# Opening, low parts and closing of a one-layer hybrid encoder: packed first loads, a set operand order, fewer column sums

## The chip, the cores and the metric

The kernel runs on one core of a Trainium2 chip. The metric is the device time of one execution in microseconds. The time before is the median of three runs.

## The reference

One encoder layer over x of 512 positions by 1024 channels, all in float32. What is computed:

```python
def rms_norm(x, g):
    y = xf * lax.rsqrt(jnp.mean(xf * xf, axis=-1, keepdims=True) + EPS)
    return y * g

def swiglu(h, w_gate, w_up, w_down):
    return (jax.nn.silu(h @ w_gate) * (h @ w_up)) @ w_down

x = x + 0.5 * swiglu(rms_norm(x, ffn1_norm), ffn1_w_gate, ffn1_w_up, ffn1_w_down)   # F = 2752
h = rms_norm(x, mix_norm)
u = h @ w_in                       # fourier 512 | q 8x64 | k 2x64 | v 2x64
f_out = fourier_mixer(u[..., :512], fnet_w, fnet_b)
a_out = gqa_attention(q, k, v, q_norm, k_norm)
x = x + jnp.concatenate([f_out, a_out], axis=-1) @ w_out
x = x + 0.5 * swiglu(rms_norm(x, ffn2_norm), ffn2_w_gate, ffn2_w_up, ffn2_w_down)
return rms_norm(x, final_norm)
```

## The kernel before

x is kept transposed in SBUF for the whole run: eight tiles `x[k]` of 128 channels by 512 positions. Every product is made of three matmuls on rounded operands: a number is split into a high part (a rounding copy to fp32r) and a low part (the rest), and `product` (L107 to L110) adds high by high, high by low and low by high into one PSUM bank. ScalarE (ACT in the profile) makes most high parts, VectorE (DVE) most low parts (`lows`, L71). Where `rest_by_dma` is used (L89 to L92), ScalarE writes the negated high part, and a DMA queued on GpSimd (POOL) adds the source to it while it transfers.

The weights stay in DRAM and are loaded by DMAs that SyncE (SP) issues in the order of the program. The raw buffers of tag `raw` (three) and `raw_g` (two) are used in turn, so a load waits for the engine that last read its buffer.

**Order.** TensorE (PE) and SP keep the order of the program (`manual_schedule` in `in_order`, L63). ScalarE, VectorE and GpSimd get theirs from a scheduler, which places each instruction by its own estimate of time; on the chip each engine then runs its queue in that order and each instruction waits for its semaphores.

**Opening** (`opening1`, L546 to L566). Eight warm-up matmuls on zeros (`WARM`, L519) run while the first loads are under way. The norm weights `gains` come by a DMA on ScalarE's queue (L56), x in five transfers and the first gate and up weights in five (`raw_first`, L525 to L531); two small tables, `qkg` and `fb`, come by DMAs on GpSimd's queue (L542, L544). Then, for pairs of channel blocks k, `scale` makes the high and low part of x times the norm weight (`hh[k]` at L125 or L127, `hl[k]` at L128), the raw weights are split (L553, L71), and the twelve matmuls of a k go through four banks `gu0_0` to `gu0_3`, three per bank in turn. The squares for the norm (`square` at L134, `sums` at L140) are added into `acc`. Ahead of k = 6 PE takes the column sum of `acc` (`sum`, L157), ahead of k = 7 it spreads the result over the rows (`row`, L184). The norm itself is applied later, when the banks are read (`evacuate`).

**Gates 42 and 4 to 7.** Five more `gate` products follow, of eight channel blocks and 24 matmuls each: 42, which is the tail, then 4, 5, 6 and 7. The tail's down weights (`tail_weights`, `rawt`, L230 to L239) are loaded and split in the same time. The low parts of the weights of gates 4 to 7 are made by `rest_by_dma`. Between them `operands` (L244 to L262) makes seven operands `rt` for the next stage from tiles `b` and `t`, for i = 0 to 3; in the first FFN the low parts of the three taken from `b` are made by `rest_by_dma` too. The `b` tiles share the two `raw_g` buffers.

**Middle.** The down products of four groups (`down`), a seven-product scheme for the rest of gate and up (`seven`, L330), the projections, attention and Fourier mixer, the output projection, and the second FFN. The change does not touch these.

**Closing** (`closing`, L970 to L1014). The last three down products are made for positions 0 to 255 (`t0`) first, then for 256 to 511 (`t1`). During `t1` PE takes the column sums of the squares of `t0` (`column`, after the third step), and `finish` (after the eighth) spreads the result and scales the output of `t0`. After the last down product the column sums of `t1` follow, the mean and power of each column pair, `rows`, and `finish` for `t1`: VectorE scales six of the eight tiles (L965) and GpSimd two (`ready`, tiles 2 and 3, L963), and four DMAs on SP store pairs of tiles in the order 0, 2, 4, 6 (L968).

Of the kernel before, what the change touches and what calls it, by code (L numbers as in the profile page):

```python
# [6 lines left out]
F32 = mybir.dt.float32  # L7
F32R = mybir.dt.float32r
BF16 = mybir.dt.bfloat16
# [14 lines left out]
WARM = 8  # L24
# [18 lines left out]
def encoder(ctx, tc, A, out):  # L43
# [68 lines left out]
    class Norm:  # L112
# [9 lines left out]
        def scale(self, k, by=None):  # L122
            g = gains[:, self.n, k : k + 1]
            if by:
                by.tensor_scalar(out=hh[k], in0=x[k], scalar1=g, scalar2=None, op0=ALU.mult)  # L125
            else:
                nc.scalar.activation(hh[k], x[k], AF.Copy, scale=g)  # L127
            nc.vector.scalar_tensor_tensor(  # L128
                out=hl[k], in0=x[k], scalar=g, in1=asf(hh[k]), op0=ALU.mult, op1=ALU.subtract
            )  # L130
# [24 lines left out]
        def sum(self, ps, c, parts, first=True, last=True):  # L155
            for i, p in enumerate(parts):
                nc.tensor.matmul(  # L157
                    ps[:, 2 * c : 2 * c + 2], p[:, c * P : (c + 1) * P], ones,
                    start=first and i == 0, stop=last and i == len(parts) - 1,
                )  # L160
# [39 lines left out]
    def ffn(norm, after, wgu, wd, wdt, opening, closing):  # L200
# [6 lines left out]
        with tc.tile_pool(name=f"act{n_}", bufs=1) as ap, tc.tile_pool(name=f"sums{n_}", bufs=2) as sp:  # L207
# [36 lines left out]
            def operands(rp, i0, i1):  # L244
                for i in range(i0, i1):
# [279 lines left out]
    nc.sync.dma_start(out=x[0], in_=A["x"][:, 0, :])  # L525
    nc.sync.dma_start(out=raws[0][:, 0:2], in_=A["first"][0][:, 0:2])
    nc.sync.dma_start(out=raws[0][:, 2:4], in_=A["first"][0][:, 2:4])
    nc.sync.dma_start(out=x[1], in_=A["x"][:, 1, :])
    for i in range(1, KH):
        nc.sync.dma_start(out=xt[:, 2 * i : 2 * i + 2, :], in_=A["x"][:, 2 * i : 2 * i + 2, :])  # L530
        nc.sync.dma_start(out=raws[i], in_=A["first"][i])  # L531
# [10 lines left out]
    nc.gpsimd.dma_start(out=qkg, in_=A["qkg"])  # L542
    fb = cp.tile([P, 4], F32, name="fb")
    nc.gpsimd.dma_start(out=fb, in_=A["fb"])  # L544

    def opening1(gate, column, row):  # L546

        pss = [bank(f"gu0_{c}") for c in range(4)]
        for i in range(KH):
            n0.scale(2 * i, None if i else nc.vector)  # L550
            hi, lo = (slot().rearrange("p (c a b) -> p c a b", c=4, b=P) for _ in range(2))
            for c in (slice(0, 2), slice(2, 4)) if i == 0 else (slice(0, 4),):
                nc.scalar.copy(hi[:, c], raws[i][:, c])  # L553
                lows(lo[:, c], raws[i][:, c], hi[:, c])
            n0.scale(2 * i + 1)
            if i == KH - 1:
                for k in range(KD):
                    n0.sums(k)
            for k in (2 * i, 2 * i + 1):
                if k == KD - 2:  # L560
                    column()
                if k == KD - 1:
                    row()
                for c in range(4):
                    product(pss[c], hi[:, c, k % 2, :], lo[:, c, k % 2, :], hh[k], hl[k], k == 0, k == KD - 1)
        return [pss[0:2], pss[2:4]]  # L566
# [388 lines left out]
    def finish(c0, c1, row=n3.row):  # L955
# [3 lines left out]
        for k0 in range(0, KD, 2):  # L959
# [8 lines left out]
            nc.sync.dma_start(out=out[:, k0 : k0 + 2, t], in_=xt[:, k0 : k0 + 2, t])  # L968

    def closing(downs, residual):  # L970
# [4 lines left out]
        sqs = []  # L975
# [82 lines left out]
def _layout(i):  # L1058
# [13 lines left out]
    def down(w):  # L1072
# [6 lines left out]
    mix = np.concatenate([np.arange(512)] + [512 + h * HD + np.arange(HD) for t in range(4) for h in (t, t + 4)])  # L1079
    w_in = i["w_in"]  # L1080
    wgu1 = gate_up(i["ffn1_w_gate"], i["ffn1_w_up"])
    return {
        "x": i["x"][0][_order()].T.reshape(KD, P, S).transpose(1, 0, 2),
        "gains": np.stack(
            [i[n].reshape(KD, P).T for n in ("ffn1_norm", "mix_norm", "ffn2_norm", "final_norm")], axis=1
        ),
# [3 lines left out]
        "first": first(wgu1),  # L1090
# [31 lines left out]
```

## Time and profile before

| | |
|---|---|
| median of 3 runs | 880.9 us (880.14 to 881.03) |
| the profiled execution's own time | 880.02 us |
| its span in the trace | 878.0 us |
| granted TensorE clock over the span | 0.996 |
| PE busy | 862.1 us (98%) |
| DVE, ACT, POOL busy | 637.2, 459.6, 31.7 us |

The trace gives times from the start of the span. A busy share near 100% on PE does not say that each matmul is at its shortest; gaps in which PE waits are read from the list of waits and the timeline, where the bracket at the end of a row tells how long the engine was idle before it and for whom it waited. A row with x2 merges two instructions; its duration is from the start of the first to the end of the second.

### The profile page before, as it was taken

The page shows a single profiled execution, that of the slowest core. Times are in us where ns is not written, and L with a number is a line of the kernel's source. Part 1 is how long each engine was busy: PE and PEld are TensorE (multiplying, and loading weights), DVE is VectorE, ACT ScalarE, POOL GpSimd, SP SyncE. Part 2 cuts the span into 40 slices and gives each one's busy share as a digit, 9 for nine tenths or more (in the row PEclk, how much of TensorE's full clock was granted, in tenths as well). Part 3 has the DMA queues.
Part 4 walks back from the last instruction along what each step waited for, and adds up shares of the span by engine and source line. Part 5 has one row for each costly group of instructions (what it writes and reads, how often), then busy time and mean ns, then how long its engine had stood idle before and what let it go on. Part 6 is the DMA issues. An engine that isn't in the chain of part 4 may idle for free.

```text
span 878.0 us, 13599 instructions
## 1 busy us (share of the span) xinstructions
PE 862.1 (98%) x5394; PEld 768.8 (88%) x5394; DVE 637.2 (73%) x1005; ACT 459.6 (52%) x761; POOL 31.7 (4%) x37
## 2 busy tenths in 40 slices
PE   8999999999999999999999999999999999999996
PEld 5878998899989998888888888889998999889986
DVE  7697985488746837699888558987974688459553
ACT  7773664256524644667775445535652366326441
POOL 0210000000000000211000000000000000000001
PEclk9999999999999999999999999999999999999998
DMA  7873322323243113521110213232323232332212
GB/s 245 199 163 135 142 85 67 120 97 119 75 143 110 46 51 108 204 84 37 49 49 25 90 63 136 84 132 97 109 78 126 95 118 78 102 115 84 73 37 96
DMA packets 31328, 89.25 MB, mean 102 GB/s; under 512 B 3616, under 2 KB 9248, under 8 KB 31136
## 3 DMA queue, kind: packets, MB, share of 16 engines
q1 hardware_dynamic: 28560, 83.37, 27.9%
q0 software_dynamic: 2560, 4.99, 3.0%
q8 instruction: 42, 0.69, 0.3%
q14 instruction: 22, 0.18, 0.1%
q10 hardware_dynamic: 144, 0.02, 0.0%
HBM read 83.91 MB, written 2.10 MB: 98 GB/s over the span
## 4 chain that ended last, share of the span: by engine, by line
PE 50%; issue 39%; DVE 5%; DMA 2%; ACT 2%; POOL 0%; SPq 0%; DVEq 0%; POOLq 0%; ACTq 0%
PE r L330 11%; PE q L330 6%; PE dn L108 4%; PE dn L110 4%; PE dn L109 4%; PE p L330 3%; PE out L108 2%; PE out L110 2%; PE out L109 2%; PE gu L110 1%; PE pt L816 1%; PE gu L108 1%; PE gu L109 1%; DMA rt<-b 1%; DMA ring<-in_wgu 1%
## 5 line engine op out<-in xcount | busy, mean ns | idle before, releaser
L330 PE MATMUL r<-rt,ring 128*128 128x256 f32 x1632 | 213.2, 283 | 0.1
L330 PEld LDWEIGHTS r<-rt,ring 128*128 128x128 f32 x1632 | 201.8, 188 | 2.6 <-ACT u L338 0.3
L108 PE MATMUL dn<-at,ring 128*128 128x512 f32 x303 | 119.7, 395 | 0.0
L109 PE MATMUL dn<-at,ring 128*128 128x512 f32 x303 | 119.6, 395 | 0.0
L110 PE MATMUL dn<-at,ring 128*128 128x512 f32 x303 | 119.6, 395 | 0.0
L330 PE MATMUL q<-rt,ring 128*128 128x256 f32 x816 | 107.9, 281 | 0.0
L330 PEld LDWEIGHTS q<-rt,ring 128*128 128x128 f32 x816 | 101.6, 188 | 0.0
L416 DVE SCALAR_TENSOR_TENSOR xt<-dn,xt 128x512 f32<-128x512 f32 x61 | 41.9, 688 | 80.1 <-PE dn L110 80.1
L71 DVE TENSOR_TENSOR ring<-s,ring 128x1024 fp32r<-128x1024 f32 x68 | 82.8, 1220 | 17.8 <-PE r L330 10.8
L100 ACT CAST ring<-raw_dn 128x768 fp32r<-128x768 f32 (+1 forms) x59 | 45.5, 775 | 95.2 <-PE dn L109 80.7
L291 ACT CAST ring<-s 128x1024 fp32r<-128x1024 f32 x68 | 71.4, 1050 | 40.3 <-PE r L330 18.3
L110 PEld LDWEIGHTS dn<-at,ring 128*128 128x128 f32 x303 | 57.0, 188 | 13.6
L109 PEld LDWEIGHTS dn<-at,ring 128*128 128x128 f32 x303 | 57.0, 188 | 13.0
L108 PEld LDWEIGHTS dn<-at,ring 128*128 128x128 f32 x303 | 57.0, 188 | 13.0
L71 DVE TENSOR_TENSOR ring<-raw_dn,ring 128x768 fp32r<-128x768 f32 (+1 forms) x59 | 51.7, 879 | 6.8 <-ACT ring L100 5.8
L71 DVE TENSOR_TENSOR ring<-raw_g,ring 128x1024 fp32r<-128x1024 f32 x34 | 41.6, 1222 | 17.0 <-PE p L330 11.0
L330 PE MATMUL p<-rt,ring 128*128 128x256 f32 x408 | 53.9, 281 | 0.0
L330 PEld LDWEIGHTS p<-rt,ring 128*128 128x128 f32 x408 | 50.8, 188 | 0.0
L291 ACT CAST ring<-raw_g 128x1024 fp32r<-128x1024 f32 x34 | 35.7, 1049 | 22.4 <-PE r L330 8.0
L300 ACT CAST ring<-raw_u 128x512 fp32r<-128x512 f32 x34 | 21.1, 621 | 37.1 <-PE dn L110 17.9
L110 PE MATMUL gu<-ring 128*128 128x512 f32 x96 | 37.9, 395 | 2.6 <-DMA ring<-in_wgu 1.8
L108 PE MATMUL gu<-ring 128*128 128x512 f32 x96 | 37.9, 395 | 0.8 <-ACT ring L553 0.7
(324 smaller groups left out, 1574.0 us busy)
## 6 DMA issues: line engine op xcount, KB each, us to landing
raw_dn<-in_wd SPq DMA_DIRECT2D x48, 384.0 KB, 3.0
raw_g<-in_wgu SPq DMA_DIRECT2D x34, 512.0 KB, 3.7
raw_u<-in_wgu SPq DMA_DIRECT2D x34, 512.0 KB, 4.4
raw_gu<-in_wgu SPq DMA_DIRECT2D x14, 512.0 KB, 3.5
raw_o<-in_wo SPq DMA_DIRECT2D x8, 512.0 KB, 3.5
raw_dn<-in_wd SPq DMA_DIRECT2D x16, 192.0 KB, 2.4
raw_in<-in_wins SPq DMA_DIRECT2D x6, 512.0 KB, 3.7
raw_f<-in_winf SPq DMA_DIRECT2D x4, 512.0 KB, 3.6
```

The lines of the kernel that those rows point to most:

```text
L71: nc.vector.tensor_tensor(out=lo, in0=src, in1=asf(hi), op=ALU.subtract)
L100: nc.scalar.copy(hi[:, :n, :], raw[:, :n, :])
L108: nc.tensor.matmul(ps, whi, mhi, start=first, stop=False)
L109: nc.tensor.matmul(ps, whi, mlo, start=False, stop=False)
L110: nc.tensor.matmul(ps, wlo, mhi, start=False, stop=last)
L291: nc.scalar.copy(hi, src)
L300: nc.scalar.copy(hi, src)
L330: nc.tensor.matmul(ps, a[:, ks], b[:, i], start=first and i == 0 and o == 0, stop=i == KH - 1 and o == 2, skip_group_check=not first,)
L416: nc.vector.scalar_tensor_tensor(out=x[d][:, t], in0=ps[:, t], scalar=0.5, in1=x[d][:, t], op0=ALU.mult, op1=ALU.add)
L816: nc.tensor.transpose(pt[:, c * P : (c + 1) * P], prob[t, b, c][:, kc * P : (kc + 1) * P], ident)
```

## The change

Opening: `gains` and x become one SBUF tile `gx`. The norm weights stand at the head of x's first transfer, and each transfer of x and of the first weights reads one contiguous piece of DRAM. `qkg` and `fb` move from GpSimd's queue to SP's: in the built program `qkg` stands between the last transfer of x and the fourth of the first weights, `fb` behind that. ScalarE and VectorE follow the order of the program inside `opening1`; the casts and low parts of all the first weights are made in halves (the very first in quarters on ScalarE), and each pair's squares and their adds come one pair later. In the built program the squares of k = 6 and 7 stand on ScalarE behind the cast of `rawt`. PE takes the twelve matmuls of a k in the order high by high over the four banks, then high by low, then low by high. Seven warm-up matmuls instead of eight.

`operands`: for i = 0 and 1 the low parts from `b` are made by VectorE (`lows`) instead of `rest_by_dma`. In the built program this leaves GpSimd's queue with the low parts of gates 4, 5, 6, 7 and then those of i = 2 and 3; before, the two of i = 0 and 1 stood ahead of gate 6's, and that of i = 2 ahead of gate 7's.

Closing: all three squares of `t0` are added into `acc` by VectorE, so that the column sum there has two matmul instructions instead of six (each shows as two rows in the trace); `column` moves from the third to the fifth step, `finish` from the eighth to the ninth. The column sums of `t1` go into one bank and get one mean. Six matmuls on the identity (`awake`) stand between the last sums. The stores go in the order 0, 4, 2, 6, the one of tiles 2 and 3 from ScalarE's queue.

```diff
-WARM = 8
+WARM = 7
...
-    gains = cp.tile([P, 4, KD], F32, name="gains")
-    nc.scalar.dma_start(out=gains, in_=A["gains"])
-    xt = cp.tile([P, KD, S], F32, name="xt")
+    gx = cp.tile([P, 4 * KD + KD * S], F32, name="gx")
+    gains = gx[:, : 4 * KD].rearrange("p (n k) -> p n k", k=KD)
+    xt = gx[:, 4 * KD :].rearrange("p (k s) -> p k s", s=S)
...
-                        if src is t or n_:
+                        if src is t or i < 2 or n_:
                             lows(l, src, h)
                         else:
                             rest_by_dma(l, h, src)
...
+    cut = [0] + [4 * KD + k * S for k in (1, 2, 4, 6, 8)]
+    def load_x(i):
+        a, b = cut[i : i + 2]
+        src = A["x"][a * P : b * P].rearrange("(p n) -> p n", p=P)
+        nc.sync.dma_start(out=gx[:, a:b], in_=src)
+    load_x(0)
+    for c in range(2):
+        nc.sync.dma_start(out=raws[0][:, 2 * c : 2 * c + 2], in_=A["first0"][c])
+    load_x(1)
     for i in range(1, KH):
-        nc.sync.dma_start(out=xt[:, 2 * i : 2 * i + 2, :], in_=A["x"][:, 2 * i : 2 * i + 2, :])
-        nc.sync.dma_start(out=raws[i], in_=A["first"][i])
+        load_x(i + 1)
+        nc.sync.dma_start(out=raws[i], in_=A["first"][i - 1])
...
-    nc.gpsimd.dma_start(out=qkg, in_=A["qkg"])
-    nc.gpsimd.dma_start(out=fb, in_=A["fb"])
...
+        with tc.manual_schedule(engines={mybir.EngineType.Activation, mybir.EngineType.DVE}):
+            for i in range(KH):
+                a, b = 2 * i, 2 * i + 1
+                halves = slice(0, 2), slice(2, 4)
+                n0.scale_high(a, None if i else nc.vector)
+                for c in (0, 1, halves[1]) if i == 0 else halves:
+                    nc.scalar.copy(hi[:, c], raws[i][:, c])
+                n0.scale_high(b)
+                n0.scale_low(a)
+                for c in halves:
+                    lows(lo[:, c], raws[i][:, c], hi[:, c])
+                n0.scale_low(b)
+                if i:
+                    sums(i - 1)
+                if i == KH - 1:
+                    sums(i)
+                for k in (a, b):
+                    if k == KD - 2:
+                        column()
+                    if k == KD - 1:
+                        row()
+                    passes = [(c, w, m) for w, m in ((hi, hh), (hi, hl), (lo, hh)) for c in range(4)]
+                    if k == 0:
+                        passes = passes[0:2] + passes[4:6] + passes[2:4] + passes[8:10] + passes[6:8] + passes[10:]
...
+        nc.sync.dma_start(out=qkg, in_=A["qkg"])
+        nc.sync.dma_start(out=fb, in_=A["fb"])
...
-        for k0 in range(0, KD, 2):
+        for k0 in (0, 4, 2, 6):
...
-            nc.sync.dma_start(out=out[:, k0 : k0 + 2, t], in_=xt[:, k0 : k0 + 2, t])
+            queue = nc.scalar if k0 in ready else nc.sync
+            queue.dma_start(out=out[:, k0 : k0 + 2, t], in_=xt[:, k0 : k0 + 2, t])
...
+    def awake(n):
+        unit = ident.bitcast(BF16)
+        ps = bank("awake")
+        for _ in range(2 * n):
+            nc.tensor.matmul(ps[:, : 2 * P], unit[:, :P], unit, start=True, stop=True)
...
-            sq = n3.square(d, t0)
-            if d == downs[0][0]:
-                more(sq, t0)
-            else:
-                sqs.append(sq)
+            more(n3.square(d, t0), t0)
...
-                if i == 3:
-                    n3.column([n3.acc, *sqs], 0, 2)
-                if i == 8:
+                if i == 5:
+                    n3.column([n3.acc], 0, 2)
+                if i == 9:
                     finish(0, 2)
...
-        pss = [bank(f"ss3_{c}") for c in (2, 3)]
-        for c, pc in zip((2, 3), pss):
-            n3.sum(pc, c, [n3.acc, sq], last=False)
+        pc = bank("ss3_2")
+        for c in (2, 3):
+            n3.sum(pc, c, [n3.acc], first=c == 2, last=False, skip_group_check=True)
+        awake(1)
+        for c in (2, 3):
+            n3.sum(pc, c, [sq], first=False, last=False, skip_group_check=True)
         residual(KD - 1, ps, t1)
         sq = n3.square(KD - 1, t1)
-        for c, pc in zip((2, 3), pss):
-            n3.sum(pc, c, [sq], first=False)
-        for c, pc in zip((2, 3), pss):
-            n3.mean(pc, c, c + 1)
+        for c in (2, 3):
+            n3.sum(pc, c, [sq], first=False, last=c == 3, skip_group_check=True)
+        awake(2)
+        n3.mean(pc, 2, 4)
```

The host's layout function packs the inputs to match; no arithmetic of the layer is moved there.

More of the change, by code (lines that the diff above doesn't have):

```diff
@@ L127, in scale, with scale_low @@
                 nc.scalar.activation(hh[k], x[k], AF.Copy, scale=g)
+        def scale_low(self, k):
+            g = gains[:, self.n, k : k + 1]
             nc.vector.scalar_tensor_tensor(
@@ L153, in column, with sum @@
             self.spread(c0, c1)
-        def sum(self, ps, c, parts, first=True, last=True):
+        def sum(self, ps, c, parts, first=True, last=True, **how):
             for i, p in enumerate(parts):
@@ L158, in sum @@
                     ps[:, 2 * c : 2 * c + 2], p[:, c * P : (c + 1) * P], ones,
-                    start=first and i == 0, stop=last and i == len(parts) - 1,
+                    start=first and i == 0, stop=last and i == len(parts) - 1, **how,
                 )
@@ L541, in encoder, with sums @@
     qkg = cp.tile([P, 2], F32, name="qkg")
-    nc.gpsimd.dma_start(out=qkg, in_=A["qkg"])
     fb = cp.tile([P, 4], F32, name="fb")
-    nc.gpsimd.dma_start(out=fb, in_=A["fb"])
     def opening1(gate, column, row):
         pss = [bank(f"gu0_{c}") for c in range(4)]
[L549 to L558, printed above, removed]
-            for k in (2 * i, 2 * i + 1):
[L560 to L565, printed above, removed]
+        def sums(i):
+            for k in (2 * i, 2 * i + 1):
+                n0.sums(k)
@@ L974, in closing @@
         t0, t1 = slice(0, S // 2), slice(S // 2, S)
-        sqs = []
         def more(sq, t):
@@ L1079, in _layout @@
     mix = np.concatenate([np.arange(512)] + [512 + h * HD + np.arange(HD) for t in range(4) for h in (t, t + 4)])
+    x = np.concatenate(
+        [
+            *(i[n].reshape(KD, P).T for n in ("ffn1_norm", "mix_norm", "ffn2_norm", "final_norm")),
+            i["x"][0][_order()].T.reshape(KD, P, S).transpose(1, 0, 2).reshape(P, KD * S),
+        ],
+        axis=1,
+    )
     w_in = i["w_in"]
@@ L1082, in _layout @@
     return {
[L1083 to L1086, printed above, removed]
+        "x": np.concatenate([p.reshape(-1) for p in np.split(x, [4 * KD + k * S for k in (1, 2, 4, 6)], axis=1)]),
         "qkg": np.stack([np.concatenate([i[n][half]] * 2) for n in ("q_norm", "k_norm")], axis=1),
@@ L1089, in _layout @@
         "fw": i["fnet_w"].transpose(1, 0, 2).reshape(P, S),
-        "first": first(wgu1),
+        "first": first(wgu1)[1:],
+        "first0": first(wgu1)[0].reshape(P, 2, 2, 2, P).transpose(1, 0, 2, 3, 4),
         "wgu1": wgu1,
```

16 lines of the change are left out of this document (11 added, 5 removed).

## The prediction

> **What bounds the kernel now.** I read the page first, then PE's list of waits, then the timeline of the stages that the change touches.
>
> ```profile
> PE 862.1 (98%) x5394; PEld 768.8 (88%) x5394; DVE 637.2 (73%) x1005; ACT 459.6 (52%) x761; POOL 31.7 (4%) x37
> ```
>
> PE is busy for 98% of the span, so an edit counts only where it takes a PE gap away, takes instructions off PE, or shortens what lies ahead of PE's first and behind its last matmul. The change does all three. In the first 90 us PE waited for this:
>
> ```profile
> PE gu L110 <- DMA ring<-in_wgu: 1.8, 1, 1.8
> ...
> PE gu L110 <- DVE ring L71: 0.7, 1, 0.7
> PE gu L108 <- ACT ring L553: 0.7, 1, 0.7
> ```
>
> The last two lie in the opening, the first is gate 7's. PE's rows of the opening:
>
> ```profile
> 1.23 3.58 PE L520 MATMUL busy<-idle 128*128 128x512 bf16 x8 [1.23 <-DVE halves L536]
> 5.46 0.51 PE L108 MATMUL gu<-ring 128*128 128x512 f32 x1 [0.65 <-ACT ring L553]
> ...
> 7.54 0.50 PE L108 MATMUL gu<-ring 128*128 128x512 f32 x1
> ...
> 13.59 0.50 PE L110 MATMUL gu<-ring 128*128 128x512 f32 x1 [0.73 <-DVE ring L71]
> 13.93 0.39 PE L108 MATMUL gu<-ring 128*128 128x512 f32 x1
> 14.16 0.40 PE L109 MATMUL gu<-ring 128*128 128x512 f32 x1
> ...
> 24.32 0.95 PE L157 MATMUL ss<-ones,acc 128*128 128x2 f32 x8
> ```
>
> A fed matmul of 512 columns starts 0.23 us after the one before it (13.93 to 14.16), and 0.34 after one that had waited (13.59 to 13.93). The column sum stands behind 72 matmuls, so fed without a gap from 5.46 it would stand at 5.46 + 72 x 0.23 = 22.0. It stands at 24.32: the gaps cost 2.3 us. From there PE runs without a gap to gate 7.
>
> **The opening, by unchanged landings.** What feeds PE:
>
> ```profile
> 3.08 0.43 SPq L531 DMA_DIRECT2D raw_first<-in_first  x1
> 4.79 0.62 ACT L553 CAST ring<-raw_first 128x512 fp32r<-128x512 f32 x1
> 6.87 0.62 ACT L553 CAST ring<-raw_first 128x512 fp32r<-128x512 f32 x1 [1.46 <-DMA raw_first<-in_first]
> 9.59 1.41 DVE L128 SCALAR_TENSOR_TENSOR ring<-xt,gains,ring 128x512 fp32r<-128x512 f32 x2
> 10.00 1.14 ACT L134 ACTIVATE sq<-xt 128x512 f32<-128x512 f32 x2
> 12.32 1.22 DVE L71 TENSOR_TENSOR ring<-raw_first,ring 128x1024 fp32r<-128x1024 f32 x1
> 20.18 0.69 DVE L140 TENSOR_TENSOR acc<-acc,sq 128x512 f32<-128x512 f32 x1
> 21.47 1.05 ACT L234 CAST ring<-rawt 128x1024 fp32r<-128x1024 f32 x1 [2.02 <-DMA rawt<-in_wdt]
> ```
> ```profile
> DMA to landing us min/median/max: 6.9/6.9/6.9
> ```
>
> The second answer is for the load issued at 3.08, which lands at 9.98. The new first matmul needs a quarter cast in place of the half at 4.79, about 0.3 earlier; but the fifth matmul now needs the half cast at 6.87, so it starts at 7.54 as bank 2's first did. Behind it eight of k = 0 remain: k = 1 starts at 7.54 + 0.34 + 7 x 0.23 = 9.49. The weights of k = 2 land at 9.98, and two half casts of 0.62 are done by 11.2; they are due at 9.49 + 12 x 0.23 = 12.3. The low parts are due eight matmuls later than the high ones, so the wait at 13.59 goes. PE arrives at the column sum at 9.49 + 60 x 0.23 = 23.3.
>
> What is late next is `acc`. From the first half cast (10.6) DVE has six low halves (half of 1.22 each), five `hl` (0.70 each, from the x2 row), seven adds (0.69) and one low part of 1.22 ahead of the sum: 3.7 + 3.5 + 4.8 + 1.2 = 13.2 by durations, some 12.5 as neighbouring rows overlap by up to 0.1, so `acc` is ready between 23.1 and 23.8. I take 23.5, a gain of 0.8 (24.32 - 23.5).
>
> **The opening, by faster landings.** The loads run slowly just when PE needs them:
>
> ```profile
> 4.00:5.00 1.00, 0.81 (x2) 0.00 (x0) 0.65 (x2) 0.84 (x2) 0.00 (x0) 1.00 0.70 164
> 5.00:6.00 1.00, 0.54 (x2) 0.37 (x2) 1.00 (x2) 0.41 (x1) 0.00 (x0) 1.00 0.89 260
> 6.00:7.00 1.00, 0.96 (x4) 0.67 (x4) 0.19 (x1) 0.13 (x1) 0.00 (x0) 1.00 0.91 317
> 7.00:8.00 1.00, 0.89 (x4) 0.30 (x3) 0.48 (x1) 0.92 (x2) 0.00 (x0) 1.00 1.05 422
> ```
> ```profile
> 2.08 0.56 POOL L544 DMA_DIRECT2D fb<-in_fb  x1
> ```
> ```profile
> fb<-in_fb POOLq DMA_DIRECT2D x1, 2.0 KB, 4.4
> ```
>
> The last number of a row is GB/s. From 4 to 7 us 741 KB moved; at 422 GB/s it would have been 1266 KB, so every later load is 525 / 422 = 1.2 us late. `fb` on GpSimd's queue is under way until 2.08 + 4.4 = 6.5, as long as the slow stretch lasts. From 7 us the remaining x loads run fast with the same strides, so I lay the slowness to GpSimd's small transfers more than to the layout. The change moves them to SP, behind all of x. Then landings come up to 1.2 us earlier, with them PE (22.1) and `acc` (22.3): a gain of 2.0. The bounds are 0.8 and 2.0; I take 2.0, by the coincidence in time. Below 0.8 the term falls only by the clock rival or a late `rawt`, both below.
>
> **The clock.** The eight warm-ups took 0.43 us each (3.58 for eight with the last one's tail), the matmuls after them 0.23. Seven last 3.0 us instead of 3.4.
>
> The Trainium skill, "TensorE: Matmul & The Clock Gate", section "What's actually happening", says the clock doubles only after one window of about 3.4 us of sustained activity. By it seven might be too few; the trace has no run with seven, so it neither agrees nor disagrees. By the rule the time would be that of the clock rival below.
>
> **Gate 7.**
>
> ```profile
> 35.71 2.60 POOL L92 DMA_DIRECT2D rt<-b  x2 [0.59 <-DVE t L255]
> 42.16 0.40 PE L108 MATMUL gu<-ring,at 128*128 128x512 f32 x1
> 42.27 1.41 DVE L248 SCALAR_TENSOR_TENSOR b<-xt,gains,rp 128x512 f32<-128x512 f32 x2 [3.29 <-DMA rt<-b]
> 48.06 1.06 ACT L91 ACTIVATE ring<-ring 128x1024 fp32r<-128x1024 f32 x1
> 49.41 0.91 POOL L92 DMA_DIRECT2D ring<-in_wgu  x1 [0.83 <-ACT ring L91]
> 53.43 0.39 PE L109 MATMUL gu<-ring 128*128 128x512 f32 x1
> 55.59 0.50 PE L110 MATMUL gu<-ring 128*128 128x512 f32 x1 [1.77 <-DMA ring<-in_wgu]
> ```
>
> Gate 7's low part was due at 53.43 + 0.23 = 53.66 and came at 55.59; with the 0.11 of a restart the gap costs 2.04. Its DMA was issued at 49.41, because ScalarE negated the high part only at 48.06, behind work on `b` for i = 2 that had waited 3.29 us for the DMAs of i = 0. With those made by VectorE the wait goes, and GpSimd issues gate 7's DMA ahead of those of i = 2 and 3. What is late next: its buffers come free when PE leaves gate 4 (42.16, then 2.0 earlier: 40.2). A cast, a cast for `b` and the negation, three ScalarE instructions of about 1 us, end by 43.2; from issue to landing it took 55.59 - 49.41 = 6.2. So it lands by 49.4 and is due at 53.66 - 2.0 = 51.7: a cover of 2.3 us, beyond which each us is a us lost. The whole gap goes: 2.04.
>
> VectorE's price is two more low parts of 768 columns:
>
> ```profile
> 841.15 1.82 DVE L71 TENSOR_TENSOR ring<-raw_dn,ring 128x768 fp32r<-128x768 f32 x2
> ```
>
> 1.8 us, in a stretch where it had waited 3.3; so VectorE is not later than before by its clock, but PE is 4 us earlier. That is the third rival.
>
> **The closing.**
>
> ```profile
> 860.43 0.28 PE L157 MATMUL ss<-ones,acc 128*128 128x2 f32 x2
> ...
> 861.68 0.37 PE L108 MATMUL last<-at,ring 128*128 128x256 f32 x1
> ```
> ```profile
> 870.90 2.44 DVE L965 SCALAR_TENSOR_TENSOR xt<-xt,gains,rp 128x256 f32<-128x256 f32 x6 [1.58 <-PE rp L196]
> ```
> ```profile
> 871.80 1.41 POOL L963 TENSOR_TENSOR xt<-xt,rb 128x256 f32<-128x256 f32 x2 [1.70 <-ACT rb L197]
> ```
> ```profile
> 873.71 0.96 SPq L968 DMA_DIRECT2D out_y<-xt  x2
> ```
>
> Six sum instructions (twelve rows) hold PE from 860.43 to 861.68, 1.25 us; two take a third, so PE is 0.84 earlier. The two extra adds on VectorE end before the fifth step, to which the sum moves. In the end part the sums of `t1` are as many as before, the merged mean waits for the same last matmul, and `awake` fits into PE's waits: nothing. The last two stores were issued one behind the other, 0.48 each, the last from about 874.2, because SP had stood behind tiles 2 and 3, which GpSimd finished at 873.2; VectorE was done at 870.90 + 2.44 = 873.34. With ScalarE issuing for GpSimd's tiles, SP's last can go at 873.4, up to 0.83 earlier; but then two transfers run side by side. Bounds 0 and 0.83; I take 0.4, most of one issue.
>
> **Sum.** 2.0 + 2.04 + 0.84 + 0.4 = 5.3. The profiled execution took 880.02, which gives 874.7; the median of the runs shown, 880.9, lies 0.88 above it and gives **875.6**.
>
> **Rivals.**
>
> *The landings do not change* (the packing and the moved tables do nothing). For: small transfers are few bytes. Against: the coincidence above. Opening 0.8: 880.9 - 4.1 = 876.8.
>
> *The clock stays at half* for another stretch as long as the eight warm-ups, 3.4 us from the first real matmul at about 5.3. PE makes 8 matmuls by 8.7 instead of 15: 7 x 0.23 = 1.6 lost, of which 0.3 is hidden by `acc`. Opening 0.7: 876.9.
>
> *A new wait behind gate 7*: VectorE or the loads late for the down products, with PE 4 us earlier. It would give back about as much as gate 7's gap, 2.0: 877.6.
>
> *Slower: the column sum waits for `rawt`.* In the new order of ScalarE the last two squares stand behind the cast of `rawt`, and PE's column sum waits for them in its fixed order; everything behind it on PE waits too. From the landing of `rawt` it is a cast (1.05), two squares (1.14) and an add (0.69) to the sum: 2.9. In the trace `rawt` landed at 21.47; in the new order its buffer comes free earlier. Up to a landing at 19.4 nothing is lost (19.4 + 2.9 = 22.3); beyond it each us costs one, and from a landing at 24.7 the gain of 5.3 is gone. Against: only a load 3 us later than before does that. Landing at 27, the time is 883.2.
>
> **Chances and range.** A measurement of this kernel can tell about 0.2% (1.8 us) from no change. Forecast 0.46, unchanged landings 0.22, clock 0.12, new wait 0.08, slower by `rawt` 0.04; the remaining 0.08 is several of the rivals together, which give 878 to 880, 0.05 of it above 879.1. So faster 0.91, same 0.05, slower 0.04. The range goes down to 874.2: the other 0.43 of the stores, 0.5 for runs as far below the median as the lowest shown and 0.5 of the opening's first cast and overlap. Up it takes in the new wait with 0.7 more: 878.3.
>
> **What would show it.** Right: the column sum near 22.3, no PE gap in gate 7, PE's last down product about 4.9 us earlier in the span, the last store issued right after VectorE's last row. Landings: over 380 GB/s from 4 us on. Clock: starts 0.43 apart after the first real matmul. `rawt`: a PE wait ahead of the column sum of over 0.5 us. Wrong altogether would be a gap of over 1 us between the column sum and the first `seven` step.

## The result, and the profile after

The changed kernel takes 876.86 us (median of six, 875.07 to 877.52) against 880.52 for the kernel before on the same chip: ratio 0.9954, 95% interval 0.9939 to 0.9968. The forecast was 875.6, the range 874.2 to 878.3. The total came out close, but the fall is 3.7 us by the medians where 5.3 was forecast, and two of its four terms did not come out as forecast.

The profiled execution took 877.47 us, its span 875.7. PE is still busy for 98% of it:

```profile
PE 862.0 (98%) x5391; PEld 769.1 (88%) x5391; DVE 640.8 (73%) x1011; ACT 459.0 (52%) x763; POOL 27.8 (3%) x33
```

PE's waits in the first 90 us (us in total, times, longest):

```profile
PE gu L595 <- ACT ring L575: 1.4, 2, 0.8
PE busy L528 <- DVE halves L552: 1.2, 1, 1.2
PE ss L165 <- DVE acc L148: 0.9, 1, 0.9
```

Gate 7's wait (1.8 us) is gone. A wait that the kernel before did not have stands in its place: the column sum `ss` waits 0.9 us for `acc`. PE's timeline of the opening:

```profile
5.01 1.27 PE L595 MATMUL gu<-ring 128*128 128x512 f32 x4 [0.62 <-ACT ring L575]
7.10 10.26 PE L595 MATMUL gu<-ring 128*128 128x512 f32 x44 [0.82 <-ACT ring L575]
17.20 5.75 PE L595 MATMUL gu<-ring,at 128*128 128x512 f32 x24
23.86 1.05 PE L165 MATMUL ss<-ones,acc 128*128 128x2 f32 x8 [0.91 <-DVE acc L148]
24.77 4.58 PE L595 MATMUL gu<-ring,at 128*128 128x512 f32 x12
29.19 0.60 PE L192 MATMUL rp<-ident,wide 128*128 128x128 f32 x4
```

The twelve products behind the sum take 4.58 us; twelve starts 0.23 apart with the last one's tail would be 2.9. The windows of 1 us show why (granted clock in the third column from the right):

```profile
24.00:25.00 1.00, 1.00 (x9) 1.00 (x10) 1.00 (x2) 0.45 (x1) 0.00 (x0) 0.96 0.32 127
25.00:26.00 1.00, 1.00 (x3) 0.77 (x3) 0.29 (x2) 0.80 (x1) 0.59 (x1) 0.50 0.06 16
26.00:27.00 1.00, 1.00 (x4) 0.74 (x3) 0.43 (x1) 0.97 (x2) 0.43 (x1) 0.50 0.58 111
27.00:28.00 1.00, 1.00 (x4) 0.81 (x3) 0.00 (x0) 0.34 (x1) 0.35 (x1) 0.50 0.96 389
28.00:29.00 1.00, 1.00 (x5) 0.77 (x5) 0.00 (x0) 0.00 (x0) 0.76 (x1) 0.83 0.80 201
```

TensorE ran at half clock for 0.08 + 3 + 0.34 = 3.4 us, which costs half of that, 1.7 us. The starts of PE's rows (before, after) give the account of the two profiled executions:

| PE reaches | before | after | difference, and its part |
|---|---|---|---|
| column sum | 24.32 | 23.86 | -0.46, the opening |
| first transposition behind it | 28.01 | 29.19 | +1.18: +1.64, half clock |
| first `seven` step | 81.14 | 80.25 | -0.89: -2.07, gate 7 |
| first `last` product | 852.95 | 852.15 | -0.80: +0.09 |
| last transposition | 870.15 | 868.51 | -1.64: -0.84, column sums of the end |
| end of the span | 878.0 | 875.7 | -2.3: -0.66, the stores |
| own time | 880.02 | 877.47 | -2.55: -0.25, outside the span |

The rows behind three of these. Gate 7's DMA was issued 3.1 us earlier (46.34 for 49.41), and in 5.7 us it landed:

```profile
46.34 0.88 POOL L93 DMA_DIRECT2D ring<-in_wgu  x1 [5.18 <-ACT ring L92]
...
ring<-in_wgu POOLq DMA_DIRECT2D x1, 512.0 KB, 5.7
```

The sum in the closing holds PE from 860.35 to 860.71, 0.36 us where it was 1.25:

```profile
860.35 0.50 PE L165 MATMUL ss<-ones,acc 128*128 128x2 f32 x4
860.71 0.37 PE L109 MATMUL last<-at,ring 128*128 128x256 f32 x1
```

The last store on SP is issued as VectorE's last row ends (869.26 + 2.44 = 871.70), next to one on ScalarE's queue:

```profile
869.26 2.44 DVE L1000 SCALAR_TENSOR_TENSOR gx<-gx,rp 128x256 f32<-128x256 f32 x6 [1.58 <-PE rp L204]
...
870.16 1.94 SPq L1004 DMA_DIRECT2D out_y<-gx  x3
...
871.59 0.45 ACTq L1004 DMA_DIRECT2D out_y<-gx  x1
```

The loads from 4 to 7 us, where the forecast wanted over 380 GB/s (last number), sum up to 1019 KB for 741 before:

```profile
4.00:5.00 1.00, 0.39 (x1) 0.00 (x0) 0.75 (x1) 0.45 (x2) 0.00 (x0) 1.00 1.06 334
5.00:6.00 1.00, 0.99 (x4) 0.67 (x4) 0.69 (x1) 0.26 (x1) 0.00 (x0) 1.00 0.85 320
6.00:7.00 1.00, 0.28 (x2) 0.00 (x0) 0.00 (x0) 0.57 (x1) 0.00 (x0) 1.00 1.01 365
```

Why `acc` came late stands in the timelines of ScalarE and VectorE, and in the landing of one load, that of the weights of k = 2 and 3, issued at 3.07:

```profile
DMA to landing us min/median/max: 6.8/6.8/6.8
```
```profile
9.87 1.14 ACT L575 CAST ring<-raw_first 128x512 fp32r<-128x512 f32 x2 [0.51 <-DMA raw_first<-in_first]
...
18.68 1.03 ACT L101 CAST ring<-raw_gu 128x1024 fp32r<-128x1024 f32 x1
19.62 0.62 ACT L142 ACTIVATE sq<-gx 128x512 f32<-128x512 f32 x1
20.17 1.05 ACT L242 CAST ring<-rawt 128x1024 fp32r<-128x1024 f32 x1
21.12 0.62 ACT L142 ACTIVATE sq<-gx 128x512 f32<-128x512 f32 x1
22.24 0.63 ACT L142 ACTIVATE sq<-gx 128x512 f32<-128x512 f32 x1 [0.50 <-DVE acc L148]
...
10.52 1.29 DVE L72 TENSOR_TENSOR ring<-raw_first,ring 128x512 fp32r<-128x512 f32 x2 [0.38 <-ACT ring L575]
...
12.71 0.69 DVE L148 TENSOR_TENSOR acc<-acc,sq 128x512 f32<-128x512 f32 x1 [0.23 <-ACT sq L142]
...
20.39 1.22 DVE L72 TENSOR_TENSOR ring<-raw_gu,ring 128x1024 fp32r<-128x1024 f32 x1
21.52 2.28 DVE L148 TENSOR_TENSOR acc<-acc,sq 128x512 f32<-128x512 f32 x3
```

In the kernel before, this load took 6.9 us from 3.08, so it hardly landed earlier. ScalarE casts it as soon as it is there, and VectorE starts on its low halves at 10.52. From the row at 12.71 on VectorE never waits again, up to the end of the last add at 21.52 + 2.28 = 23.80; the sum starts at 23.86. In this row the low part of the tail gate's weights, which PE needs only from 32 us on, takes 1.22 us ahead of the last three adds. ScalarE casts the same weights and those of `rawt` between the last squares, but that did not hold up these adds: the square of 19.62 was done at 20.24, and the add that takes it began at 21.52; the last square itself waited 0.5 us for an add to free its buffer. A fed PE would have stood at the sum 1.1 us earlier: 23.86 less the 1.31 since the last product's start, plus 0.23.

### The profile page after: what moved, and what is told of

Read it like the earlier page. It is cut to its first block, busy times and chain, and to the rows that moved or that the text cites. A ratio compares the mean times of both kernels' runs of the same rounds, so it can differ in the third digit from the quotient of the medians.

```text
span 875.7 us, 13587 instructions
## 1 busy us (share of the span) xinstructions
PE 862.0 (98%) x5391; PEld 769.1 (88%) x5391; DVE 640.8 (73%) x1011; ACT 459.0 (52%) x763; POOL 27.8 (3%) x33
## 4 chain that ended last, share of the span: by engine, by line
PE 94%; ACT 2%; DVE 2%; DMA 1%; issue 1%; SPq 0%; POOL 0%; DVEq 0%; ACTq 0%
PE r L338 22%; PE q L338 11%; PE dn L109 8%; PE dn L111 8%; PE dn L110 8%; PE p L338 6%; PE gu L109 3%; PE gu L111 3%; PE gu L110 3%; PE out L109 2%; PE out L111 2%; PE out L110 2%; PE pt L851 1%; PE q L109 1%; PE q L110 1%; PE q L111 1%
## 5 line engine op out<-in xcount | busy, mean ns | idle before, releaser
L424 DVE SCALAR_TENSOR_TENSOR gx<-dn,gx 128x512 f32<-128x512 f32 x61 | 42.1, 690 | 82.0 <-PE dn L111 82.0
L383 DVE TENSOR_TENSOR u<-g,u 128x512 f32<-128x512 f32 x34 | 23.4, 688 | 15.9 <-ACT u L382 15.9
L109 PE MATMUL gu<-ring 128*128 128x512 f32 x80 | 31.3, 392 | 0.0
```

What stands on the lines that cost most here:

```text
L109: nc.tensor.matmul(ps, whi, mhi, start=first, stop=False)
L383: nc.vector.tensor_tensor(out=u, in0=b["g"], in1=u, op=ALU.mult)
L424: nc.vector.scalar_tensor_tensor(out=x[d][:, t], in0=ps[:, t], scalar=0.5, in1=x[d][:, t], op0=ALU.mult, op1=ALU.add)
```

## The experiments

In the kernels that change the opening, the line numbers of the profile differ by a few.

**1. Later weights behind the last squares.** Theory: the order on ScalarE and VectorE makes `acc` late, and the wait brings the half clock.

```diff
+def column():                       # called ahead of k = 6, inside the set order
+    held.append(weights(wgu[2 * NF], ...))      # tail gate
+    tail_weights()
+    held.append(weights(wgu[4], ..., by_dma=True))
+    norm.column([norm.acc])
...
+sums(KH - 1); column()              # the squares come ahead of these casts
```

> The changed kernel, but ScalarE casts the weights of the tail gate and of the down tail after the last two squares instead of between them, and VectorE makes the tail gate's low part after the last add. Theory: in the changed kernel the column sum stood 1.1 us late (23.86 where a fed PE would be at 22.8) because these casts lay ahead of the last squares, and the wait then cost a stretch of 3.4 us at half clock in about half of the executions (those at 877.4 with a mean clock of 0.996, against 875.7 with 0.998). Then here the column sum is at 22.8, no matmul of 512 columns after it starts 0.43 behind the one before, every execution has a mean clock of 0.998, and the median is 875.7 - 1.1 = 874.6. Rival 1: the sum waits for the loads of x or for VectorE's own work; then it stays near 23.9 and the median near 876.9. Rival 2: the half clock comes from the seven warm-ups or from elsewhere; then the stretch is still there in about half of the executions and the median is near 875.7.

Measured: 875.28 (874.33 to 875.61), ratio 0.9933 (0.992 to 0.9947). PE's timeline:

```profile
22.66 1.05 PE L165 MATMUL ss<-ones,acc 128*128 128x2 f32 x8
23.58 3.05 PE L587 MATMUL gu<-ring,at 128*128 128x512 f32 x12
27.02 0.66 PE L192 MATMUL rp<-ident,wide 128*128 128x128 f32 x4 [0.40 <-DVE wide L184]
```

The wait and the slow products are gone (3.05 for twelve). Of the 1.1 us only part arrives (874.6 was expected): the transpositions now wait 0.4 us, because VectorE forms the mean behind the low parts that were moved. Rival 2 falls, and rival 1 by its number (23.9 for the sum). But its cause, VectorE's own work, is the one that the rows bear out: the edit moved ScalarE's casts and VectorE's low part together, and the low part counted. VectorE's row from the first low half of k = 2 to the last add now takes 12.34 us (10.27 to 22.61) for 13.28 in the changed kernel (10.52 to 23.80), 0.94 less, by the low part that is gone from it:

```profile
19.53 3.08 DVE L148 TENSOR_TENSOR acc<-acc,sq 128x512 f32<-128x512 f32 x4
```

The other 0.25 us is the earlier start of the row. The mean clocks were 0.996 to 0.999, not 0.998 throughout as expected; experiment 3 shows why the mean clock is no sure sign of a stretch at the sum.

**2. The wait filled with spare matmuls.** Theory: it is PE's idleness that halves the clock.

```diff
 if k == KD - 2:
+    for _ in range(8):
+        nc.tensor.matmul(spare[:, : 2 * P], unit[:, :P], unit, start=True, stop=True)
     column()
```

> The changed kernel with eight spare bf16 matmuls of 256 columns ahead of the column sum, about 0.9 us of PE's time, so that PE works through the wait. Theory (the idle stretch at the column sum brings the half clock): the column sum stays at 23.9, the half clock is gone from every execution, mean clock 0.998 throughout, median 875.7. Rival (the half clock does not depend on PE being idle there): some executions still have a mean clock of 0.996 and the median stays near 876.9.

Measured: 875.46 (875.14 to 876.73).

```profile
22.62 1.05 PE L589 MATMUL spare<-ident 128*128 128x256 bf16 x8
23.50 0.95 PE L165 MATMUL ss<-ones,acc 128*128 128x2 f32 x8
24.32 3.04 PE L598 MATMUL gu<-ring,at 128*128 128x512 f32 x12
```

The sum is hardly earlier than in the changed kernel (23.50 for 23.86), yet the products behind it run at full clock, and no execution is above 876.8. The rival predicted some of them and a median of 876.9. The profile alone does not settle it: `acc` was ready at 23.3 here, so that without the spare matmuls PE would have idled some 0.6 us, and after idle times of 0.63 to 0.77 us the profiles of experiments 7, 8 and 10 show no slow products either. What speaks for the theory is that none of the five executions is in the upper group.

**3. The two low parts alone**, in the kernel before.

```diff
-if src is t or n_:
+if src is t or i < 2 or n_:
```

> The kernel before with one edit of the change: VectorE makes the low parts of b for i = 0 and 1. Theory: the gap of gate 7 goes and nothing takes its place: 2.0 us less, 878.5 by the median of 880.5. Rival (a new wait behind gate 7, because VectorE has 1.8 us more to do): a PE gap of 1 to 2 us between gate 7 and the first seven step, and 880 to 880.5.

Measured: 878.11 (878.06 to 879.27), ratio 0.9969 (0.9958 to 0.9979), so 1.9 to 3.7 us less. PE has no wait between 14 us and the first `seven` step, and gets from the transpositions (28.32) to it (79.38) in 51.06 us, where the kernel before took 53.13: 2.07 less. That the median moved by some 0.9 more is within the interval. Three of the 17 executions of the kernel before lie above 882 with a mean clock of 0.993 to 0.994, so a stretch at half clock may cost it time too, at gate 7 or elsewhere; no profile shows where. This run's own profile shows one such place, at the end:

```profile
868.31 2.08 PE L196 MATMUL rp<-ident,r 128*128 128x128 f32 x8 [1.02 <-POOL r L171]
```

The clock was halved from 867.9 us on, and the last transpositions take 2.08 us, where they take 1.16 in every other profile. This is the only stretch at half clock in it behind the warm-up, and the mean clock of this execution is 0.995, lower than the 0.996 of the changed kernel's profile with its stretch at the sum. So the mean clock does not tell whether there was a stretch at the sum.

**4. The end alone**, in the kernel before (the edits from `finish` on).

```diff
-for k0 in range(0, KD, 2):
+for k0 in (0, 4, 2, 6):
...
+queue = nc.scalar if k0 in ready else nc.sync
...
-n3.column([n3.acc, *sqs], 0, 2)
+n3.column([n3.acc], 0, 2)
...
```

> The kernel before with the edits of the end alone: column sums over one tile, the merged mean, the spare matmuls, the order of the stores and the two stores on ScalarE's queue. The prediction's terms: 0.84 on PE and 0.4 at the stores, 1.24 together: 879.3. What the two profiles show (0.84 up to the last transposition, then 0.9 more to the end): 1.75, 878.8. If the end part gained only what PE gained: 879.7.

Measured: 879.81 by 881.04, ratio 0.9988 (0.998 to 0.9997): 0.3 to 1.8 us less. The interval tells neither 1.24 from 1.75 nor either from the 0.84 of PE alone (the last of the three values expected, 879.7, lies nearest). From the last transposition (869.72) to the end of the span (876.9) it took 7.18, as in the changed kernel (7.19), against 7.85 before: the stores are worth 0.67.

**5. The sum six matmuls later.** Theory: work ahead of the wait takes it away for good.

```diff
-if k == KD - 2: column()
-if k == KD - 1: row()
...
+if k == KD - 2 and n == 6: column()    # within the twelve matmuls of k
+if k == KD - 1 and n == 6: row()
```

> The changed kernel with the column sum and the transpositions behind it six matmuls of 512 columns (1.4 us of PE) later, so that PE has work until the sum's tile is ready. Theory: the wait at the column sum (1.1 us) goes, and unlike in the first experiment nothing waits at the transpositions (there PE stood 0.5 us at them, because VectorE formed the mean only after the low parts); first matmul of the tail gate about 1.1 us earlier than in the changed kernel's unslowed executions: 874.6. Rival: the transpositions, or what needs the row factors behind them, become late instead; then 875.3, as in the first experiment.

Measured: 875.92 (874.78 to 876.67). The theory's 874.6 missed; the rival's late stage came, but further on. The sum waits 0.2 us, nothing waits at the transpositions, and then:

```profile
63.70 0.50 PE L112 MATMUL dn<-at,ring 128*128 128x512 f32 x1 [1.20 <-DVE ring L73]
```

The down products wait 1.2 us for VectorE. This is the prediction's rival of a new wait behind gate 7. It does not occur in the changed kernel as it stands, but it takes what this placement had won.

**6. The small loads back on GpSimd's queue.**

```diff
+nc.gpsimd.dma_start(out=qkg, in_=A["qkg"])     # beside their tiles
+nc.gpsimd.dma_start(out=fb, in_=A["fb"])
...
-nc.sync.dma_start(out=qkg, in_=A["qkg"])       # behind all of x
-nc.sync.dma_start(out=fb, in_=A["fb"])
```

> The changed kernel with the two small loads (qkg, fb) back on GpSimd's queue at the start. The prediction's cause (these transfers slow the loads between 4 and 7 us): the loads fall back from 1019 KB to about 741 KB in these 3 us, the second half cast of the first weights starts near 6.9 instead of 6.43, PE's long run near 7.5 instead of 7.10, and the median rises by about 0.4 to 877.3. Rival (the slow stretch came from the strided layout of x and of the first weights): the rate stays near 1019 KB, the half cast near 6.4, and the median near 876.9.

Measured: 877.58 (876.47 to 879.28). Windows of 1 us and PE's timeline:

```profile
4.00:5.00 1.00, 0.82 (x2) 0.41 (x2) 0.86 (x2) 0.71 (x2) 0.00 (x0) 1.00 0.75 207
5.00:6.00 1.00, 1.00 (x3) 0.83 (x3) 0.56 (x1) 0.00 (x0) 0.00 (x0) 1.00 0.60 198
6.00:7.00 1.00, 0.65 (x2) 0.00 (x0) 0.00 (x0) 0.00 (x0) 0.00 (x0) 1.00 0.96 375
```
```profile
8.23 12.92 PE L597 MATMUL gu<-ring 128*128 128x512 f32 x44 [1.58 <-ACT ring L577]
```

From 4 to 7 us 780 KB came in. The second half cast started at 7.56 instead of 6.43, PE's long run at 8.23 instead of 7.10, and its 44 products took 12.92 us instead of 10.26: having waited 1.58 us, PE started its products 0.43 us apart until 13.9 and 0.23 apart from there on. That is the stretch at half clock that the clock rival named, here behind a wait. (The clock column of these windows reads 1.00 ahead of the first change on record, the rise at 13.9, and says nothing about them.) The execution profiled, 879.28, is the slowest of the six; by the ratios, 0.9965 (0.9952 to 0.9977) here, 0.9954 (0.9939 to 0.9968) and, in experiment 9, 0.9935 (0.9919 to 0.995) for the changed kernel, a loss of time is likely and its size open. One more number was not expected: time less span is 2.13 to 2.21 in all six executions, against 1.73 to 1.82 in the twelve of the changed kernel. The two loads may be part of what the changed kernel gained outside the span (0.25), but not by themselves: with them moved and the end as before (experiment 8) it is 1.93 to 1.98. And in experiment 3, which left these loads where they were and changed only the low parts, it is 2.16 to 2.21 against 2.00 to 2.10 in the kernel before beside it.

**7. Strided loads.** The packing undone, all else as changed.

```diff
-src = A["x"][a * P : b * P].rearrange("(p n) -> p n", p=P)
+src = A["x"][:, a:b]
```

> The changed kernel with x and the first weights laid out in DRAM as before, so that each transfer reads strided rows. The prediction's cause (GpSimd's small transfers): no difference, about 1019 KB from 4 to 7 us and 876.9. Rival (the layout): the rate falls back towards 741 KB, the half cast to 6.9, the median to 877.3.

Measured: 876.46 (875.13 to 880.14), with this in the windows:

```profile
4.00:5.00 1.00, 0.81 (x3) 0.30 (x3) 0.88 (x3) 0.71 (x2) 0.00 (x0) 1.00 0.86 238
5.00:6.00 1.00, 0.85 (x4) 0.37 (x3) 0.56 (x1) 0.00 (x0) 0.00 (x0) 1.00 1.04 379
6.00:7.00 1.00, 0.22 (x1) 0.23 (x2) 0.24 (x1) 0.81 (x2) 0.00 (x0) 1.00 0.99 358
```

975 KB, and the half cast at 6.11: the layout did nothing that shows. Experiments 6 and 7 speak for the prediction's cause, with one profile each. Over all 14 profiles, the rate from 4 to 7 us is 247 to 278 GB/s in the four with the small loads on GpSimd's queue and 268 to 361 in the ten without, seven of them at 325 and above; the load of k = 2 and 3 lands 6.9 to 7.6 us after its issue in the four and 5.5 to 7.2 in the ten. The ranges overlap, so this is a tendency and not a law.

**8. The opening alone**, in the kernel before: the closing and the line of experiment 3 put back as they were.

```diff
-if src is t or i < 2 or n_:
+if src is t or n_:
...
-n3.column([n3.acc], 0, 2)
+n3.column([n3.acc, *sqs], 0, 2)
...
```

> The kernel before with the opening's edits alone (gate 7's gap and the end as before). The prediction's term: 2.0 us less, 879.0 by a median of 881.0. What the changed kernel's profile shows: PE reaches the column sum 0.5 us earlier and about half of the executions lose 1.7 us to the half clock behind it; between 878.5 (with all that is gained outside PE's rows) and 881.

Measured: 880.97 by 880.88, ratio 1.000 (0.999 to 1.001): no difference, within 0.9 us either way. PE's waits in the first 100 us:

```profile
PE dn L111 <- DVE at L72: 1.1, 1, 1.1
PE gu L111 <- DMA ring<-in_wgu: 0.7, 1, 0.7
PE ss L165 <- DVE acc L148: 0.6, 1, 0.6
```

PE reached the transpositions at 27.10, 0.9 earlier than before, but the first `seven` step at 80.57, only 0.57 earlier. Gate 7's wait shrank to 0.7 and a wait of 1.1 in the down products opened behind it.

**9. The changed kernel again**, unchanged.

> The changed kernel, unchanged, to see how often the half clock behind the column sum costs an execution 1.7 us. Theory: two groups again, near 875.7 and near 877.4, with about half of the executions in each (three of six so far), and the median between. Rival (the three at 877.4 were something else, such as one bad chip or call): all near 875.5, as in the experiments that took PE's idle time at the sum away (ten executions, none above 876.8).

Measured: 876.66, ratio 0.9935 (0.9919 to 0.995) to 882.73 for the kernel before on this chip; three executions at 875.36 to 875.78 and three at 877.54 to 878.67. The profiled one (878.23) is of the upper group and shows the same picture, with a longer wait, because the load of k = 2 and 3 took 7.2 us to land (VectorE's row runs from 10.97 to 24.25, again 13.28):

```profile
24.31 1.05 PE L165 MATMUL ss<-ones,acc 128*128 128x2 f32 x8 [1.85 <-DVE acc L148]
25.22 4.60 PE L595 MATMUL gu<-ring,at 128*128 128x512 f32 x12
```

Six of the twelve executions of the changed kernel lie above 877.3. In experiments 1, 2, 11 and 12, where PE does not idle at the sum, it is none of twenty (the highest is 877.07). That the six had the half clock at the sum is read from two profiles, both of the upper group, and from the times; the other four were not profiled. The 877.07, of experiment 11, has a mean clock of 0.994, lower than any of the twelve (0.995 to 0.998), so a stretch at half clock can fall elsewhere too.

**10. Eight warm-ups** (`WARM = 8`), all else as changed.

> The changed kernel with eight warm-up matmuls instead of seven. If seven are as good as eight: the first product starts up to 0.2 us later in executions where the first weights land early, and the median is that of the changed kernel run beside it, plus 0 to 0.2. Rival (with seven, the clock stays at half for another stretch in some executions, 0.5 to 1.7 us each): fewer executions above 877, the median 0.5 to 1 us below that of the changed kernel.

Measured: 875.98 (875.12 to 877.15), ratio 0.9926 (0.9913 to 0.9939); the changed kernel on the same chip 876.66 and 0.9935. The intervals overlap: inconclusive. PE waited 0.77 us at the sum in this profile, and the twelve products behind it took 3.02 us, without a slow stretch.

**11. The mean ahead of the low parts**, on top of experiment 1.

```diff
+norm.mean(ps, 0, 4)
+norm.power(0, 4)
 tail_weights()
 held.append(weights(wgu[4], ..., by_dma=True))
-norm.column([norm.acc])
+norm.spread(0, 4)
```

> The first experiment's kernel (casts of later weights behind the last squares) with one more move: VectorE forms the mean before the low parts of the down tail instead of behind them. Theory: the transpositions no longer wait (they came at 27.02 there, 0.5 after PE could have started them), so the work behind them starts 0.5 to 0.7 us earlier: 874.6 by 875.28. Rival (the stretch behind has no slack left: the down products wait for VectorE as when the sum was placed later, where 1.4 us came back at 63.70): no gain, 875.3 to 876.

Measured: 874.92 (874.56 to 877.07), ratio 0.9917 (0.9902 to 0.9931); the changed kernel on the same chip 876.66. The gain is between theory and rival. PE runs from 6.56 us on without a wait up to the first `seven` step:

```profile
22.40 1.05 PE L165 MATMUL ss<-ones,acc 128*128 128x2 f32 x8
23.32 3.03 PE L594 MATMUL gu<-ring,at 128*128 128x512 f32 x12
26.19 0.60 PE L192 MATMUL rp<-ident,wide 128*128 128x128 f32 x4
```

By medians this is the fastest version, 1.7 us below the changed kernel; the intervals of the two ratios still touch (up to 0.9931 here, from 0.9919 there).

**12. Experiments 10 and 11 together.**

> The eleventh kernel (casts of later weights behind the last squares, the mean ahead of the down tail's low parts) with eight warm-ups instead of seven: the two edits that came out fastest, together. If they add, the first products run at the full clock (in the eleventh kernel's profile it came only at 5.37, so three of them started 0.43 to 0.59 apart): 0.3 to 0.6 us less, 874.4. If the wait for the second half of the first weights (6.55 there) ends the opening either way: 874.9, no difference.

Measured: 875.35 (874.41 to 875.51), ratio 0.9921 (0.9907 to 0.9934). Both values expected, 874.4 and 874.9, were missed. No gain over experiment 11 shows, on another chip; in the profile the wait for the second half of the first weights (1.2 us, PE resumes at 7.31) sets the opening.

## Why the prediction was right, and where it was not

**Gate 7: right in place and size.** Forecast 2.04; the two profiles give 2.07, and alone it gives 2.07 by its rows (experiment 3). DMA issue before the loads of i = 2 and 3, cover sufficient: as told.

**Closing: right.** Forecast 0.84, measured 0.84. The spare matmuls and the merged mean: nothing between the two profiles, as told. But the half clock that caught the last transpositions in experiment 3 (0.9 us) was in one of the three profiles with the old closing and in none of the eleven with the new one; whether the spare matmuls prevent it is not shown.

**Stores: undersized.** Forecast 0.4 in bounds of 0 to 0.83; 0.66 came. The last issue came 0.84 earlier relative to the last transposition (874.21 - 870.15 = 4.06 for 871.73 - 868.51 = 3.22), the whole upper bound. Two transfers side by side took back 0.2, not half.

**Opening: wrong.** Forecast 2.0, with bounds of 0.8 and 2.0; the column sum came 0.46 earlier, and the opening alone gave nothing (experiment 8). The step that failed first is the landing, and with it `acc` at 22.3: it came at 23.80, 1.5 later.

1. The step "every later load is 525 / 422 = 1.2 us late" took a shortfall of bytes over three microseconds for the lateness of each load. More bytes did come, 1019 KB from 4 to 7 us and not 1266, and the second half cast started 0.44 earlier (6.43 for 6.87); PE, fed, would have stood at the sum at 22.8, not 22.1. But the load of k = 2 and 3, from which the prediction counted VectorE's work, landed 6.8 us after 3.07 where it had taken 6.9 from 3.08: 0.1 earlier, not 1.2. VectorE's row began at 10.52, where the forecast of 10.6 less 1.2 gives 9.4: 1.1 us of the 1.5. The cause named, GpSimd's small loads, is likely and not proved (experiments 6 and 7).
2. The "some 12.5" for VectorE's work was too small. From 10.6 to the 23.5 taken it is 12.9; the row took 13.28, and 13.27 to 13.29 in the seven other profiles with this order: the other 0.4 us. The prediction's own sum by durations, 13.2, was nearer, and its upper bound for unchanged landings, 23.8, is what came. The list of the work was right, the low part of 1.22 included. That this low part need not stand there was overlooked: behind the sum it saves 0.94 (experiment 1). The slower rival stood near this place, but `rawt` landed in time.
3. That a wait of 0.9 us would cost more than itself was not foreseen. The clock rival put the half clock at the warm-ups; it came at the column sum, 1.64 us in the profiled execution, and by the times of experiment 9 in about half of them.

**Not in the sum:** 0.25 us outside the span. It goes when the small loads are put back (experiment 6) and mostly also with the old end (experiment 8), and the low parts alone shift it the other way (experiment 3); what makes it is open.

So the total was near because the opening's shortfall (1.5, and 1.6 more where the half clock comes) was partly made up by the stores (0.26) and the part outside the span (0.25); an execution without the half clock is at 875.1 to 876.3, around the forecast of 875.6. The rival of unchanged landings gives almost the measured median (876.8) and has `acc` about right, but the median is near by luck: that rival has neither the half clock nor the larger gain at the stores. Of the signs set down beforehand, the gap at gate 7 and the last store came out; the column sum (23.86 for 22.3) and the end of PE's work (1.64 earlier by the last transposition, not 4.9) did not.

## What to carry to other kernels

Find the load at the head of the row that ends last, and take its own landing from the trace: that more bytes arrive over a stretch does not say that this load lands earlier. Then add up the row to the point where the engines meet, by durations and with the gaps between dependent rows (three adds of 0.69 took 2.28 here): a low part whose result was needed 10 us later cost 0.94 us because it stood ahead of what PE needed next. A short wait on TensorE in the middle of dense work can cost more than itself in some executions; in experiment 2 it was filled with spare matmuls. And a gain early in a chain with little slack is not a gain at the end: alone the opening gave nothing, and the profile shows the next late producers right behind it.

## What the runs showed of the hardware

PE idled 0.91 us at the sum in one profile of the changed kernel and 1.85 in the other, then did eight matmuls of 2 columns (0.9 us); both times a stretch of 3.4 us at half clock followed, though PE had run without a wait for some 16 us before. After idle times of 0.63 to 0.77 us at the same place (experiments 7, 8 and 10) no such stretch followed, nor after gate 7's wait of 1.8 us in the kernel before. The clock records of the traces put every change of the clock a whole number of 3.413 us after the first rise: the drop at the sum six of them (20.48 us) in both profiles, the drop at the end 252 to 255 of them in the kernels without it. The rise itself came at 3.97 to 6.18 us, and at 13.86 in experiment 6.

The Trainium skill, "TensorE: Matmul & The Clock Gate", section "What's actually happening", gives the half clock after at least one idle window of about 3.4 us. The length of the stretch agrees with that window; the idle time that brought it on was about half of it or less, so the measurement decides. The same section says that the window runs freely; the traces agree, with the first rise at times that differ from run to run. That is not the whole reason why one wait brings the half clock and another does not: by these records gate 7's wait (53.82 to 55.59) lay within one window (52.45 to 55.87, counted from the rise at 4.67), not split over two, and brought none. How much of a window must be idle is open.

Two transfers of 1 and 2 KB on GpSimd's queue, next to loads of 256 and 512 KB on SP's, went with 247 to 278 GB/s over 3 us in four profiles, against 268 to 361 in the ten without them (325 and above in seven). In the changed kernel they also went with 0.4 us more between the span and the time of the execution (2.13 to 2.21 for 1.73 to 1.82), but experiment 3 shows the same 2.16 to 2.21 without a change to them.
